# First expert's tokens gathered like the others, eight embedding parts ahead of the experts, and two loads of w_proj_b moved ahead

## The chip, the cores and the metric

The kernel runs on one core of a Trainium2 chip. A core has five engines, each with its own queue that it works off in order: TensorE (PE, matrix products), VectorE (DVE), ScalarE (ACT), GpSimd (POOL) and SyncE (SP). SP, ACT and POOL also issue DMA transfers, which the core's 16 DMA engines carry out. The metric is the device time of one execution in microseconds (us), here the median of several runs. The kernel before takes 1797.73 us (median of 3 runs, 1795.44 to 1806.05).

## The reference

One decoder block: 512 tokens of width 1024, in float32. Two gated linear-attention mixers are merged and projected, and the result is normalised into `x2`. Then a mixture of 32 experts, each token going to its best four, is added to a gate of per-layer embeddings `p`, and the sum is normalised:

```python
ya = o_a @ w_proj_a;  yb = o_b @ w_proj_b
merged = sigmoid(gate_a) * ya + sigmoid(gate_b) * yb
x2 = layer_norm(ALPHA * x + merged @ w_out)          # in words, shortened
top_logit, top_e = lax.top_k(x2 @ w_router + b_router, 4)
top_w = softmax(top_logit)
# for each expert e, on the tokens that chose it:
gate = minimum(hgu[:, :1024], 7.0); up = clip(hgu[:, 1024:], -7.0, 7.0)
act = (up + 1.0) * gate * sigmoid(1.702 * gate)
y += top_w * (act @ w_down[e] + b_down[e])
emb = sigmoid(x2 @ w_ple_gate) * (p @ w_ple_proj)    # 512 x 1024
out = layer_norm(ALPHA * x2 + y + emb)
```

## The kernel before, in words

**The stages.** The first 600 us are the two mixers and the merge. The merge multiplies by `w_proj_b` in two halves of 512 columns; its second half loads two 1 MB pieces (`raw`, L199) through SP, converts each piece on ACT and DVE into two parts (L172, L174) and multiplies them on PE (L182, L184). The results leave PSUM through L935 on DVE. Then `w_out` follows, and for each of the four tiles of 128 tokens the second norm: `second_norm(n)` stores the normed rows `hr` to DRAM (`h_d`, L974) and turns them into `H2` (L980); `logits(n)` (L986) and `choose` (L992 to L1007) find the four best experts of every token.

**The sort.** Experts are sorted by their number of tokens: `sort_experts` (L1128, from `key` L1131 and `tmp` L1133 on) writes each expert's rank, and for every rank a table of token numbers is made by small matmuls (`ptab`, L862) and a few steps on DVE (`tb` L864 to `gidx` L879). Ranks 0 and 1 are the first two experts by number (FIXED), so their tables hang on no ranks, but they stand behind the sort in the code.

**The 32 experts.** Nineteen are long (96 slots for tokens, as blocks of 64 and 32), thirteen short (64 slots). An expert's tokens are fetched from `h_d` by an indirect DMA of POOL (`gather`, L1326) while the expert ahead is computed, and turned by PE and ACT (`ptr`, L1342; `turned`, L1343). The weights, 12 MB for an expert, come through SP in loads of 1 MB (L1318) into 18 buffers that are reused in turn; the buffers of `hr` and `gb` are among them. Every product of the experts has line L1452: `pg` and `pq` up, `po` and `pq` down. The outputs `og` are added to `y_d` in DRAM by POOL (L1596).

**The first expert** is the exception. Its tokens are not gathered: `place(n)` (L1013, 64 matmuls) multiplies `hr` by a one-hot matrix straight into the PSUM banks `px`, which ACT copies to where the tokens belong (L1605). Its products start before the sort is done; the sort, the first tables and gather(1) are in its fourth step (TABLES_AT = 3).

**The embedding parts.** `embed(i)` computes one of 32 pieces of 128 tokens by 128 columns: 8 matmuls of `H2` with `rawg`, 2 of `pT` with `rawp` (L1037, L1039), a sigmoid on ACT (L1041) and a product on DVE (L1042) into `stg`. After four pieces a column is full and POOL adds it to `y_d` (L1044). `stg` has one buffer. Every expert computes one piece between its up and down products; experts 25 and 27 compute two, experts 30 and 31 none. `scaled_rows` (L1237) writes ALPHA times `hr` to `y_d` through a buffer `tmp` that the sort uses too.

**What sets the order.** The program is written once, in the order of the code, and a scheduler then moves instructions by their readiness in its own model; after that each engine's queue is fixed, and an instruction that has to wait holds up all behind it on its engine.

Of the kernel before, what the change touches and what calls it, by code (L numbers as in the profile page):

```python
# [21 lines left out]
P = 128  # L22
S = 512
NT = S // P
D = 1024
# [25 lines left out]

SPLIT_AHEAD = 300
# [7 lines left out]

TABLES_AT = 3
# [34 lines left out]
def block_kernel(ctx: ExitStack, tc: tile.TileContext, a: dict, out: bass.AP):  # L96
# [69 lines left out]
    low_after = []  # L166

    def split_parts(src, shape, tag="w"):
        with tc.high_priority(offset=ahead[0]):
            both = split.tile([P, 2] + shape[1:], F32R, name="parts_" + tag, tag="parts")  # L170
            hi, lo = both[:, 0], both[:, 1]
            s_.activation(hi, src, AF.Copy)  # L172
            with tc.issue_after(low_after.pop()) if low_after else nullcontext():
                v_.tensor_tensor(lo, src, f32(hi), op=ALU.subtract)  # L174
        return hi, lo
# [725 lines left out]
    M = CAP  # L901
# [23 lines left out]
    firsts = [m10[:, i, :] for i in range(4)]  # L925
    nc.sync.dma_start(gates[0], gb_d.rearrange("i p t -> p i t"))
# [5 lines left out]
    for c in range(2):  # L932
# [8 lines left out]
        project(psm, wpb[:, c * 512:(c + 1) * 512], 512, lambda k: oTb[k], "T", ev, (vt, gt) if c == 0 else ())  # L941
# [18 lines left out]
    ohs_f = ep.tile([P, K4 * NE + NT * M], F32, name="ohs_f", tag="xg")  # L960
    oh = ohs_f[:, :K4 * NE].rearrange("p (k e) -> p k e", e=NE)
    ohf = ohs_f[:, K4 * NE:].rearrange("p (n m) -> p n m", m=M)
# [25 lines left out]
    def choose(n0, n1):  # L988
# [17 lines left out]
        for n in range(n0, n1):  # L1006
            chosen = v_.tensor_scalar(ohf[:, n, :], iota_s[:, :M], pos1[:, n, 0:1], None, op0=ALU.is_equal)  # L1007
        return chosen.ins

    def place(n, halves=(0, 1)):  # L1010

        for k in range(halves[0] * 4, halves[-1] * 4 + 4):
            tc.keep_in_program_order(t_.matmul(px[k // 4][:, k % 4, :M], hr[:, n, k * P:(k + 1) * P], ohf[:, n, :],  # L1013
                                               start=False, stop=False))
# [8 lines left out]

    def embed(i):

        n = i % NT
        cs = slice(i // NT * P, (i // NT + 1) * P)
        if n == 0:
            raw = emb["gate"] = plp.tile([P, KD, P], F32, name="rawg", tag="rawg")
            nc.scalar.dma_start(raw, a["w_ple_gate"][0][:, cs].rearrange("(k q) c -> q k c", q=P))  # L1030
            rawp = emb["proj"] = plp.tile([P, 2, P], F32, name="rawp")
            nc.scalar.dma_start(rawp, a["w_ple_proj"][0][:, cs].rearrange("(k q) c -> q k c", q=P))
            emb["out"] = plp.tile([P, NT, P], F32, name="stg")
        t = slice(n * P, (n + 1) * P)
        pg = psm.tile([P, 512], F32, name="ple", tag="att")
        for k in range(KD):
            t_.matmul(pg[:, :P], H2[:, k, t], emb["gate"][:, k, :], start=(k == 0), stop=(k == KD - 1))  # L1037
        for k in range(2):
            t_.matmul(pg[:, P:2 * P], pT[:, k, t], emb["proj"][:, k, :], start=(k == 0), stop=(k == 1))  # L1039
# [61 lines left out]

    px = [psm.tile([P, 4, P], F32, name="px", tag="proj", bufs=4) for _ in range(2)]

    def frame(half, start):

        nothing, one = sel[0:1, 1:2].to_broadcast([1, P]), ones_b[0:1, 0:1].to_broadcast([1, 512])
        t_.matmul(px[half].rearrange("p k m -> p (k m)"), nothing, one, start=start, stop=not start)

    frame(0, True)
    frame(1, True)  # L1110
    choose(0, 2)
    place(0)
# [57 lines left out]
    def first_tables():  # L1170
# [3 lines left out]
        with tc.issue_after(chosen):  # L1174
            sort_experts(pc[:, :NE])
# [505 lines left out]
```

## Time and profile before

| what | us |
|---|---|
| median of 3 runs | 1797.73 |
| the profiled execution | 1802.86 |
| its span in the trace | 1801.1 |
| PE busy | 1725.2 (96% of the span) |
| DVE busy | 557.4 (31%) |
| ACT busy | 409.0 (23%) |
| POOL busy | 196.3 (11%) |

All times in the rows below count from the start of the span. A row of the timeline gives a start, a duration, the engine, the line of the kernel, the operation with its output and inputs, and how many instructions the row takes together; in square brackets stands the idle time of the engine just before it and what the engine waited for ("<-DMA ..." a transfer, "<-PE ..." another engine). The product L1452 on `turned` at 674.58 is the first of expert 0.

### The profile page before, as it was taken

To read this page: it belongs to the slowest core of one execution; us is meant where nothing else is said; L and a number is where in the kernel's file an instruction comes from. 1 tells how busy PE (TensorE), PEld (TensorE's weight loads), DVE (VectorE), ACT (ScalarE), POOL (GpSimd) and SP (SyncE) were. 2 spreads that over 40 slices of the span, in tenths; PEclk is the share of its full clock that TensorE was granted. 3 is DMA by queue.
4 is the path that set the end of the run, shared out by engine and by line. 5 is a ranking of instruction groups with operands and counts; after the bars stand their busy time and mean duration, and the time that the engine had idled before them with its cause. 6 is when DMAs were issued, how large, how long until landed. Compare 5 with 4: busy or idle time off the path is not lost. (4 is left out here: it accounts for less than half of the span.)

```text
span 1801.1 us, 26079 instructions
## 1 busy us (share of the span) xinstructions
PE 1725.2 (96%) x10591; PEld 973.9 (54%) x10591; DVE 557.4 (31%) x1326; ACT 409.0 (23%) x653; POOL 196.3 (11%) x202
## 2 busy tenths in 40 slices
PE   6999999999998999999999999999999999999994
PEld 5888887888886873344343434334343434334422
DVE  7566455436334654111121111111111102102104
ACT  3665455334322321011011011011010101101111
POOL 1000000000000101102011102102010101110113
PEclk9999999999998989999999999999999999999997
DMA  8322232322218477999999999999999998999993
GB/s 267 107 70 71 71 136 99 140 94 71 94 71 297 167 282 300 359 414 356 408 361 406 406 370 355 409 413 380 410 409 388 405 411 316 415 362 412 408 370 133
DMA packets 127642, 513.93 MB, mean 285 GB/s; under 512 B 14434, under 2 KB 44546, under 8 KB 78228
## 3 DMA queue, kind: packets, MB, share of 16 engines
q1 hardware_dynamic: 95988, 466.11, 64.6%
q0 software_dynamic: 16160, 29.63, 6.8%
q10 hardware_dynamic: 15360, 16.39, 2.7%
q8 instruction: 86, 1.41, 0.3%
q14 instruction: 48, 0.39, 0.1%
HBM read 484.36 MB, written 27.72 MB: 284 GB/s over the span
## 5 line engine op out<-in xcount | busy, mean ns | idle before, releaser
L1452 PE MATMUL pg<-raw,turned 128*64 128x512 f32 (+1 forms) x2120 | 423.2, 532 | 4.1 <-DVE up L1502 3.7
L1452 PEld LDWEIGHTS pg<-raw,turned 128*64 128x64 f32 x2120 | 149.4, 137 | 240.6 <-issue 200.9
L1502 DVE TENSOR_SCALAR up<-pg 128x256 f32<-128x256 f32 (+1 forms) x45 | 24.2, 537 | 708.2 <-PE pg L1452 708.2
L1452 PE MATMUL pq<-raw,turned 128*32 128x512 f32 (+1 forms) x2000 | 198.3, 498 | 0.0
L1452 PE MATMUL po<-raw,turned 128*64 128x512 f32 x784 | 175.9, 597 | 0.0
L182 PE MATMUL proj<-parts_w,H 128*128 128x512 f32 x640 | 161.7, 398 | 0.0
L182 PE MATMUL proj<-H,parts_w 128*128 128x512 f32 x640 | 157.4, 394 | 3.3 <-ACT vt L499 1.9
L174 DVE TENSOR_TENSOR parts_w<-raw,parts_w 128x1024 fp32r<-128x1024 f32 x84 | 102.5, 1222 | 154.5 <-ACT parts_w L172 154.0
L1500 ACT ACTIVATE sgs<-pg 128x256 f32<-128x256 f32 (+1 forms) x45 | 21.3, 474 | 543.7 <-PE pg L1452 543.7
L1596 POOL DMA_INDIRECT y_d<-og,sidx x50 | 80.0, 1600 | 526.6 <-ACT og L1587 321.7
L182 PEld LDWEIGHTS proj<-parts_w,H 128*128 128x128 f32 x640 | 121.2, 191 | 25.1 <-DVE H L939 0.3
L182 PEld LDWEIGHTS proj<-H,parts_w 128*128 128x128 f32 x640 | 119.1, 188 | 28.2 <-ACT vt L499 2.3
L172 ACT ACTIVATE parts_w<-raw 128x1024 fp32r<-128x1024 f32 x84 | 88.7, 1059 | 178.0 <-PE proj L184 172.1
L1452 PEld LDWEIGHTS pq<-raw,turned 128*32 128x32 f32 x2000 | 55.3, 109 | 124.3 <-issue 106.6
L1452 PEld LDWEIGHTS po<-raw,turned 128*64 128x64 f32 x784 | 55.1, 138 | 97.7 <-issue 93.3
L184 PE MATMUL proj<-parts_w,H 128*128 128x512 f32 x320 | 84.0, 393 | 0.0
L1326 POOL DMA_INDIRECT xg<-h_d,gidx x49 | 50.4, 1029 | 295.6 <-PE ptr L1342 248.5
L184 PE MATMUL proj<-H,parts_w 128*128 128x512 f32 x320 | 80.5, 390 | 0.0
L1587 ACT ACTIVATE og<-po,wslot 128x512 f32<-128x512 f32 x32 | 22.0, 687 | 214.1 <-PE po L1452 199.9
L184 PEld LDWEIGHTS proj<-parts_w,H 128*128 128x128 f32 x320 | 60.8, 190 | 12.9
L184 PEld LDWEIGHTS proj<-H,parts_w 128*128 128x128 f32 x320 | 59.9, 188 | 12.4
L1037 PE MATMUL ple<-rawg,H 128*128 128x128 f32 x512 | 62.4, 275 | 0.0
(351 smaller groups left out, 1800.0 us busy)
## 6 DMA issues: line engine op xcount, KB each, us to landing
raw<-in_w_gate_up_dram SPq DMA_DIRECT2D x223, 1024.0 KB
raw<-in_w_down_dram SPq DMA_DIRECT2D x98, 1024.0 KB
raw<-in_w_in_dram SPq DMA_DIRECT2D x36, 1024.0 KB
hr<-in_w_gate_up_dram SPq DMA_DIRECT2D x22, 1024.0 KB
hr<-in_w_down_dram SPq DMA_DIRECT2D x20, 1024.0 KB
gb<-in_w_gate_up_dram SPq DMA_DIRECT2D x11, 1024.0 KB
gb<-in_w_down_dram SPq DMA_DIRECT2D x10, 1024.0 KB
raw<-in_w_proj_a_dram SPq DMA_DIRECT2D x4, 1024.0 KB
```

What stands on the lines that cost most here:

```text
L172: s_.activation(hi, src, AF.Copy)
L174: v_.tensor_tensor(lo, src, f32(hi), op=ALU.subtract)
L182: t_.matmul(ps, wh if keep else x, x if keep else wh, start=st, stop=False)
L184: t_.matmul(ps, wl if keep else xh, xh if keep else wl, start=False, stop=stop)
L1037: t_.matmul(pg[:, :P], H2[:, k, t], emb["gate"][:, k, :], start=(k == 0), stop=(k == KD - 1))
L1326: g_.indirect_dma_start(out=columns_of(xg, i), out_offset=None, in_=by_parts(h2_d, parts), in_offset=bass.IndirectOffsetOnAxis(ap=gidx[:, ...
L1452: t_.matmul(dst, x, cols, start=start, stop=stop, skip_group_check=closed)
L1500: s_.activation(dst, gate, AF.Sigmoid, scale=SW_ALPHA)
L1502: v_.tensor_scalar(tmp, up, LIMIT + 1.0, 1.0 - LIMIT, op0=ALU.min, op1=ALU.max)
L1587: s_.activation(columns_of(og, i), (po, pq)[i][:, :D // parts] if i else po, AF.Copy, scale=wslot[:, e, i:i + 1])
L1596: g_.indirect_dma_start(out=by_parts(y_d, parts), out_offset=rows_of(e, i), in_=columns_of(og, i), in_offset=None, compute_op=ALU.add)
```

## The change

- **First expert.** `place`, the banks `px` and their copies are gone. The sort and the first tables come directly behind the choice of the last tile; expert 0 gets its tokens by `gather(0)` and is turned like all others.
- **Embedding parts.** The first eight (two columns) stand in the code between the first tables and expert 0, and the weights of both columns are loaded ahead (`rawg`, `rawp` have two buffers). The other 24 are spread by a formula that gives none to experts 4, 9, 14, 19, 24, 29, 30 and 31 and one to each of the rest.
- **Rows.** `scaled_rows` scales `hr` in place and stores it, without `tmp`.
- **Loads.** The two `raw` pieces of the second half of `w_proj_b` are issued by SP ahead of the loads of `m`, not behind them.
- **Room.** `oh` shrinks, and the program is built with a smaller scratch for DMA descriptors that POOL writes (8192).

The diff, cut to its core:

```diff
+EMBED_FIRST = 8
+EMBED_BUFS = 2
-TABLES_AT = 3
...
+    raws_pb = [ring.tile([P, 4, 512], F32, name="raw", tag="raw") for _ in range(2)]
+    for u in range(2):
+        nc.sync.dma_start(raws_pb[u], wpb[:, 512:].rearrange("(k p) c -> p k c", p=P)[:, 4 * u:4 * u + 4, :])
     nc.sync.dma_start(gates[0], gb_d.rearrange("i p t -> p i t"))
     nc.sync.dma_start(m10, m1_d[:4].rearrange("i p t -> p i t"))
...
-        project(psm, wpb[:, c * 512:(c + 1) * 512], 512, lambda k: oTb[k], "T", ev, (vt, gt) if c == 0 else ())
+        project(psm, wpb[:, c * 512:(c + 1) * 512], 512, lambda k: oTb[k], "T", ev, (vt, gt) if c == 0 else raws_pb)
...
     choose(0, 2)
-    place(0)
     second_norm(2)
     logits(2)
     second_norm(3)
-    place(1, (0,))
     choose(2, 3)
     logits(3)
-    place(1, (1,))
-    place(2, (0,))
-    chosen = choose(3, 4)
-    place(2, (1,))
-    low_after += [chosen] * 3
-    for half in range(2):
-        place(3, (half,))
-        frame(half, False)
+    choose(3, 4)
...
     def scaled_rows():
 
         for n in range(NT):
-            tmp = ep.tile([P, D], F32, name="tmp", tag="og")
-            s_.activation(tmp, hr[:, n, :], AF.Copy, scale=ALPHA)
-            nc.scalar.dma_start(y_d[n * P:(n + 1) * P, :], tmp)
+            s_.activation(hr[:, n, :], hr[:, n, :], AF.Copy, scale=ALPHA)
+            nc.scalar.dma_start(y_d[n * P:(n + 1) * P, :], hr[:, n, :])
...
     def embeds(e):
 
-        while len(done) < min(e + 1 + (e >= NE - 7) + (e >= NE - 5), NE):
+        while len(done) < min(EMBED_FIRST + -(-(e + 1) * (NE - EMBED_FIRST) // (NE - 2)), NE):
             embed(len(done))
             done.append(e)
...
-            if e == 0 and k == TABLES_AT:
-                first_tables()
-                xg = gather(1)
-                main_tables(2)
...
-    for half in range(2):
-        s_.activation(xs[:, half * 4:half * 4 + 4, :], px[half][:, :, :M], AF.Copy)
+    embed_weights(0)
+    embed_weights(1)
+    first_tables()
+    xg0 = gather(0)
     scaled_rows()
+    for i in range(EMBED_FIRST):
+        embed(i)
+        done.append(i)
+    turn_tokens(xg0, 0)
     for e in range(NE):
-        if e % 2 == 0 and 0 < e < NE - 2:
+        if e % 2 == 0 and e < NE - 2:
...
-    nc = bacc.Bacc("TRN2", target_bir_lowering=False, num_devices=1)
+    nc = bacc.Bacc("TRN2", target_bir_lowering=False, num_devices=1, dynamic_dma_scratch_size=8192)
```

**PE, from the choice of the last tile to the products of expert 0.** Before, the products of expert 0 (`pg`, `pq` on `turned_9427`) stand around the first matmul that needs the sort (`pord`) and around the small table matmuls (`ptab`):

```order
L1452 MATMUL pg<-raw,turned_9427 64x512 x12
L1143 LDWEIGHTS facts
L1143 MATMUL pord<-sel_by,facts 1x32
L1452 MATMUL pg<-raw,turned_9427 64x512 x4
L1452 MATMUL pq<-raw,turned_9427 32x512 x9
L862 LDWEIGHTS ohs
L862 MATMUL ptab<-facts,ohs 128x3
L1452 MATMUL pq<-raw,turned_9427 32x512
```

In the changed program the same place on PE reads as follows. The row `ptab` of 128x3 stands 32 times (16 for token numbers, 16 for weights), the pair of `ple` rows eight times and `ptab` of 128x6 sixteen times:

```order
L1122 MATMUL pord<-sel_by,facts 1x32
L861 LDWEIGHTS ohs
L861 MATMUL ptab<-facts,ohs 128x3
...
L1035 MATMUL ple<-rawg,H_9433 128x128 x8
L1037 MATMUL ple<-rawp,pT 128x128 x2
...
L1319 MATMUL ptr<-ident,xg 128x128 x6
...
L861 MATMUL ptab<-facts,ohs 128x6
L1429 MATMUL pg<-raw,turned_9427 64x512 x16
L1429 MATMUL pq<-raw,turned_9427 32x512 x16
```

Behind `pord` and in front of the embedding parts now stand all 32 table matmuls; expert 0's products stand behind the parts and behind the turning of its gathered tokens (`ptr`).

**ACT, at the last two tiles' norms.** With the semaphores that each row waits for: before, the store of the normed rows of tile 2 (`h2_d`, the DRAM rows `h_d`), the copies into `H2`, the scaled rows to `tmp`, and the same for tile 3:

```order
L974 DMA h2_d_62<-hr_9054 128x1024 [waits DMAHW0_49,DVE_49]
L980 ACTIVATE H2_9433<-pt_9806 128x4x128 [waits PE_49]
L980 ACTIVATE H2_9433<-pt_9812 128x4x128 [waits PE_49]
L1241 ACTIVATE tmp_9921<-hr_9054 128x1024 [waits DMAHW4_49]
L1242 DMA y_d_63<-tmp_9921 128x1024 [waits DMAHW2_49,Activation_49]
L974 DMA h2_d_62<-hr_9054 128x1024 [waits DVE_49]
L980 ACTIVATE H2_9433<-pt_9838 128x4x128 [waits PE_49]
```

and in the changed program:

```order
L973 DMA h2_d_62<-hr_9054 128x1024 [waits DMAHW1_49,DVE_49]
L979 ACTIVATE H2_9433<-pt_9792 128x4x128 [waits PE_49]
L979 ACTIVATE H2_9433<-pt_9798 128x4x128 [waits PE_49]
L1218 ACTIVATE hr_9054<-hr_9054 128x1024 [waits DMAHW1_49]
L973 DMA h2_d_62<-hr_9054 128x1024 [waits DMAHW4_49,DVE_49]
L979 ACTIVATE H2_9433<-pt_9824 128x4x128 [waits PE_49]
```

The scaling of tile 2 (L1218) overwrites the rows that the store of tile 2 reads, and waits for the semaphore that this store sets (DMAHW1); the copies of tile 3 stand behind it.

**ACT, at the second column of the first eight parts**, in the changed program (`stg_9997` is the first column, `stg_10051` the second, in the same buffer):

```order
L1039 ACTIVATE stg_9997<-ple_10037 128x128 [waits PE_49]
L1020 DMA rawp_10269<-in_w_ple_proj_dram 128x2x128 [waits DMAHW7_49]
L1039 ACTIVATE stg_10051<-ple_10052 128x128 [waits DMASW4_49,DVE_49,PE_49]
L1039 ACTIVATE stg_10051<-ple_10065 128x128 [waits PE_49]
L1039 ACTIVATE stg_10051<-ple_10078 128x128 [waits PE_49]
L1018 DMA rawg_11274<-in_w_ple_gate_dram 128x8x128 [waits DMAHW0_49,PE_49]
L1039 ACTIVATE stg_10051<-ple_10091 128x128 [waits PE_49]
L1320 ACTIVATE turned0_9427<-ptr_10105 128x4x2x64 [waits PE_49]
L1320 ACTIVATE turned0_9427<-ptr_10111 128x2x4x32 [waits PE_49]
```

The first sigmoid of the second column waits for DMASW4, the semaphore of the DMA by which POOL adds the first column to `y_d`; the copies of expert 0's tokens stand behind the four sigmoids. Before, one column took four experts, and no such rows stood ahead of expert 0.

## Rows read from the trace of the kernel before

**Rows 1.** Waits of PE from 720 us on, first row: total us, times, longest.

```profile
PE ptr L1342 <- DVE sgs L1504: 10.4, 10, 1.0
```

**Rows 2.** Windows: stretch, sum, engines' busy us, granted clock, DMA share, GB/s.

```profile
1025.00:1050.00 25.00, 23.96 (x140) 8.27 (x136) 3.66 (x7) 2.20 (x5) 0.00 (x0) 1.00 1.02 422
```

**Rows 3.** Waits of SP's queue from 720 us on: total us, times, longest.

```profile
SPq L1318 <- DMA rawg<-in_w_ple_gate_dram: 132.6, 7, 23.1
```

**Rows 4.** Timeline of ACT, second half of w_proj_b.

```profile
571.62 2.00 ACT L172 ACTIVATE parts_w<-raw 128x1024 fp32r<-128x1024 f32 x2 [13.91 <-PE proj L184]
574.34 1.06 ACT L172 ACTIVATE parts_w<-raw 128x1024 fp32r<-128x1024 f32 x1 [0.71 <-DMA raw<-in_w_proj_b_dram]
```

**Rows 5.** Timeline of PE, start of the second half of w_proj_b.

```profile
575.83 0.47 PE L182 MATMUL proj<-oTl,parts_w 128*128 128x512 f32 x1 [2.89 <-DVE gb L935]
...
577.41 0.63 PE L182 MATMUL proj<-oTl,parts_w 128*128 128x512 f32 x1
...
580.39 0.47 PE L182 MATMUL proj<-oTh,parts_w 128*128 128x512 f32 x1
```

**Rows 6.** Timeline of ACT, norms of tiles 2 and 3.

```profile
657.03 0.33 ACTq L974 DMA_DIRECT2D h_d<-hr  x1
...
663.40 1.09 ACT L980 ACTIVATE H<-pt 128x512 f32<-128x512 f32 x2 [3.15 <-PE pt L979]
670.87 1.06 ACT L1241 ACTIVATE tmp<-hr 128x1024 f32<-128x1024 f32 x1 [6.38 <-DMA y_d<-tmp]
```

**Rows 7.** Timeline of DVE, choice of the last tile, sort, first tables.

```profile
667.24 0.20 DVE L992 MAX8 top<-plg 128x8 f32<-128x32 f32 x1 [1.89 <-PE plg L986]
...
668.72 0.18 DVE L999 CAST mask_b<-mask 128x32 bf16<-128x32 f32 x1
...
679.96 1.22 DVE L1133 TENSOR_TENSOR tmp<-key 128x1024 f32<-128x1024 f32 x1 [5.51 <-DMA y_d<-tmp]
...
694.26 0.17 DVE L864 COPY tb<-ptab 128x12 f32<-128x12 f32 x1 [1.55 <-PE ptab L862]
```

**Rows 8.** Timeline of PE, from the last logits to expert 2, and expert 8.

```profile
663.63 1.03 PE L1013 MATMUL px<-ohs_f,hr 128*128 128x96 f32 x8
...
674.58 5.37 PE L1452 MATMUL pg<-raw,turned 128*64 128x512 f32 x24
...
696.02 0.56 PE L862 MATMUL ptab<-facts,ohs 128*128 128x3 bf16 x16
...
707.31 1.95 PE L1037 MATMUL ple<-rawg,H 128*128 128x128 f32 x16
...
709.54 0.40 PE L1342 MATMUL ptr<-ident,sgs 128*128 128x128 f32 x2
...
717.07 0.87 PE L1342 MATMUL ptr<-ident,xg 128*128 128x128 f32 x6
...
722.43 5.37 PE L1452 MATMUL pg<-raw,turned 128*64 128x512 f32 x24
...
759.17 5.32 PE L1452 MATMUL pg<-raw,turned 128*64 128x512 f32 x24
...
949.12 2.11 PE L1452 MATMUL pg<-raw,turned 128*64 128x512 f32 x8
...
988.44 4.08 PE L1452 MATMUL pg<-raw,turned 128*64 128x512 f32 x18
```

**Rows 9.** Tile y_d: waits until a transfer (us, times), and landing times.

```profile
  DMA y_d<-stg: 43.8, 5
...
DMA to landing us min/median/max: 8.3/9.6/16.3
```

**Rows 10.** Tile stg: landing of its own transfers, as far as seen.

```profile
DMA to landing us min/median/max: 16.3/16.3/16.3
```

**Rows 11.** Timeline of DVE and of PE, one embedding part in a short expert.

```profile
1350.40 0.42 DVE L1504 SCALAR_TENSOR_TENSOR sgs<-pg,sgs 128x256 f32<-128x256 f32 x1
...
1351.82 0.40 PE L1342 MATMUL ptr<-ident,sgs 128*128 128x128 f32 x2
```

More of the change, by code (lines that the diff above doesn't have):

```diff
@@ L1 @@
 import math
-from contextlib import ExitStack, nullcontext
+from contextlib import ExitStack
 import concourse.bass as bass
@@ L172, in split_parts @@
             s_.activation(hi, src, AF.Copy)
-            with tc.issue_after(low_after.pop()) if low_after else nullcontext():
-                v_.tensor_tensor(lo, src, f32(hi), op=ALU.subtract)
+            v_.tensor_tensor(lo, src, f32(hi), op=ALU.subtract)
         return hi, lo
@@ L959, in block_kernel @@
     nc.gpsimd.dma_start(ptile, a["p"][0, 0].rearrange("(n q) d -> q n d", q=P))
[L960 to L962 removed]
+    oh = ep.tile([P, K4, NE], F32, name="oh", tag="xg")
     ohv = oh.rearrange("p (n k) e -> p n e k", n=NT)
@@ L1005, in choose @@
                                 op0=ALU.add, op1=ALU.mult)
[L1006 to L1014, printed above, removed]
     wos = {}
@@ L1022, in block_kernel, with embed_weights @@
     emb = {}
+    def embed_weights(c):
+        cs = slice(c * P, (c + 1) * P)
+        raw = plp.tile([P, KD, P], F32, name="rawg", tag="rawg", bufs=EMBED_BUFS)
+        nc.scalar.dma_start(raw, a["w_ple_gate"][0][:, cs].rearrange("(k q) c -> q k c", q=P))
+        rawp = plp.tile([P, 2, P], F32, name="rawp", bufs=EMBED_BUFS)
+        nc.scalar.dma_start(rawp, a["w_ple_proj"][0][:, cs].rearrange("(k q) c -> q k c", q=P))
+        emb[c] = raw, rawp
     def embed(i):
-        n = i % NT
-        cs = slice(i // NT * P, (i // NT + 1) * P)
+        n, c = i % NT, i // NT
+        cs = slice(c * P, (c + 1) * P)
+        if c not in emb:
+            embed_weights(c)
         if n == 0:
[L1029 to L1032, printed above, removed]
             emb["out"] = plp.tile([P, NT, P], F32, name="stg")
+        gate, proj = emb[c]
         t = slice(n * P, (n + 1) * P)
@@ L1100, in block_kernel @@
         add_out(0, {n: ps[n]})
[L1102 to L1110, printed above, removed]
     choose(0, 2)
-    place(0)
     second_norm(2)
@@ L1468, in rows_down @@
             return wd_e[:, 2 * u * P:(2 * u + 2) * P, :].rearrange("o (p j) d -> p (o j) d", j=2)
-        xg = gather(e + 1) if 0 < e < NE - 1 else None
+        xg = gather(e + 1) if e < NE - 1 else None
         first, *more = blocks(e)
@@ L1546, in expert @@
         if e == NE - 2:
-            lasts["bias"] = plp.tile([P, D], F32, name="bb3", tag="rawg")
+            lasts["bias"] = plp.tile([P, D], F32, name="bb3", tag="rawg", bufs=EMBED_BUFS)
             lasts["gain2"] = plp.tile([P, NT, P], F32, name="stg").rearrange("p n c -> p (n c)")
@@ L1553, in expert @@
             spread(lasts["bias"], a["ln_moe_b"][0])
-        while len(done) < min(e + 1 + (e >= NE - 7) + (e >= NE - 5), NE):
-            embed(len(done))
-            done.append(e)
+        embeds(e)
         if not last:
```

9 lines of the change are left out of this document (3 added, 6 removed).

## The prediction

> **What bounds the kernel now.** I read the windows first, then the waits of PE, then the timelines around the two places that the change touches. In the stretch of the experts PE is busy almost all the time, 23.96 of 25 us in a typical window, and the DMA engines are at a share of 1.02 there [rows 2]: PE is the bound, the weight stream runs close behind it. Yet the waits of PE from 720 us on name no weight load; the longest row is 10.4 us behind DVE's `sgs` [rows 1]. So work taken from PE inside the experts shortens the kernel as long as the loads keep up. Ahead of the experts it is otherwise: there a chain of choice, sort, tables and transfers decides when expert 0 can start, and today PE passes over it, since expert 0 starts at 674.58 while the sort begins at 679.96 only [rows 7, 8].
>
> **The change, step by step. Times are on the clock of the profiled execution.**
>
> *w_proj_b.* PE stands still for 2.89 us at 575.83 behind L935 on DVE [rows 5]. DVE is late because it converts pieces that ACT could only take at 571.62, and the next at 574.34, when the load landed [rows 4]. The idle time of 13.91 at 571.62 is put down to PE, but three buffers for parts had come free by then, so I take this for the first piece's landing. Loads issued ahead of `m` land earlier; what stays is the emptying of one PSUM bank, some 0.7 us by estimate, so 2.2 of the 2.89 go. Behind the idle time seven matmuls from 577.41 to 580.39 last up to 0.63 and need 2.98 us, twice the usual, that is the lower of PE's two clock levels [rows 5]; without the idle time 1.5 more go. Gain 3.7; the bounds are nothing and 4.4 (all idle time and the clock). PE is busy from there to the logits, so what is won here arrives at them.
>
> The two pieces came 2.7 us apart [rows 4], close to the 2.5 us that 1 MB takes at the 422 GB/s of [rows 2], so they came one behind the other and not mixed with all else; that is why I let them profit from an earlier place. The Trainium skill, page "DMA: Bandwidth & Descriptors", section "Issuing engines are not separate DMA queues", says that transfers of SP, ACT and POOL run on the same 16 engines and interleave whoever starts them. By that, POOL's loads issued in the same microseconds would keep the pieces late; the gain would be nothing and the sum below 3.7 us higher.
>
> *ACT at tile 3.* Scaling in place waits for the store of tile 2, issued at 657.03 [rows 6]. Stores to `y_d` land after 8.3 to 16.3 us, median 9.6 [rows 9]; I take 9.6, so the scaling can start at 666.6. It takes 1.06, and the copies of tile 3 stand behind it and behind another issue of 0.33: they start at 668.0 instead of 663.40 [rows 6]. From there to the choice on DVE were 3.84 us [rows 6, 7], of which `place` held PE for 1.03 [rows 8]. The choice comes at 670.9 instead of 667.24. Bounds: 669.6 (landing in 8.3), and 666.2 if the store is done before.
>
> *Sort and tables.* The mask is done 1.66 after the choice [rows 7]; counting and `key` I put at 0.5. The sort's `tmp` no longer waits for `y_d<-tmp` (5.51 idle before it [rows 7]) and starts at 673.1, 6.9 earlier than now. From `tmp` to the table copy `tb` are 14.3 us, of which 1.55 is a wait for table matmuls stuck between products of expert 0 [rows 7]; they are alone now, so `tb` comes at 685.8. The last 16 table matmuls end 2.3 after it (696.02 with 0.56 against 694.26 [rows 7, 8]): 688.1. From some 671 to there PE has almost nothing: this is the cost of giving up `place`.
>
> *The eight parts.* In PE's new order they stand behind all 32 table matmuls, so they cannot fill that hole. One part is 2.23 us, 707.31 to 709.54 [rows 8]; eight are 17.8, and 1.5 more for the low clock after the idle time (the same as at 577 us [rows 5]). PE ends them at 707.5. Gather(0) is hidden under them: issued at some 688, even 16.3 us [rows 9] would bring it by 705. But the fourth part ends at 698.5, sigmoid and product take 0.6 by estimate, and then POOL adds the first column to `y_d`; the first sigmoid of the second column waits for that, and behind it on ACT stand the copies of expert 0's tokens. This transfer is seen to land once, in 16.3 us [rows 10]; POOL's later transfers waited for such ones 43.8/5 = 8.8 us on average [rows 9], and stores to `y_d` have the median 9.6. With the weight buffers full, little else is moved then, so I take 10.2: landing at 709.3. Four sigmoids, transposes (0.87 for six of them [rows 8]) and the copies add some 2.8: expert 0 starts at 712.1. Less the 3.7 from above that is 708.4, **33.8 later than 674.58.**
>
> *Expert 0.* It becomes like expert 1. Today 674.58 to 722.43 is 47.85, expert 1 to 759.17 is 36.74 [rows 8]: **minus 11.1.** Hidden tables and 3 us of waits for the sort are in this.
>
> *Parts among the experts.* Eight are gone. The six in short experts (4, 9, 14, 19, 24, 29) covered a wait: `sgs` is done at 1350.82, the transposes behind the part start at 1351.82 [rows 11], so at least 1.0 of 2.23 goes; the next bias products move into the gap, so I take 1.35 each, 8.1 (bounds 6.0 and 13.4). The second parts in experts 25 and 27 stood behind a first one and covered nothing: 4.5. **Minus 12.6.**
>
> *Order of products.* Expert 8, 949.12 to 988.44, is 39.3 because PE changes between `pg` and `pq` at every weight piece, 2.6 more than expert 1 with the same work [rows 8]. In the new order it runs nearly like expert 1; others change little. **Minus 2.5** (bounds 0 and 3).
>
> *Free.* Scaling in place costs ACT what `tmp` did, hidden after the choice. The weights of the first two columns are loaded ahead, during the sort. The smaller descriptor scratch: bounds nothing and one wait of POOL for a transfer, 8.8 us [rows 9], which is hidden under an expert for each gather but the first; I take nothing.
>
> **Sum.** 33.8 - 11.1 - 12.6 - 2.5 = +7.6. On the profiled execution's 1802.86 that is 1810.5; it lies 5.1 above the median of 1797.73, so against the median I predict **1805**, 0.4% above, which a measurement of this kernel hardly tells from no change (about 1% is what it can).
>
> **The rivals.**
>
> *The weight stream becomes the bound (slower).* Behind expert 1 the change makes PE 15.1 us faster (12.6 + 2.5), while the DMA share is already 1.02 [rows 2], and SP's loads waited 132.6 us for semaphores shared with slow `rawg` loads [rows 3], which remain. If nothing of the 15.1 is kept, the sum is 33.8 - 11.1 = +22.7: 1820, 1.3% slower. It counts as slower once 10.4 of the 15.1 come back as waits of PE. Against it: PE waits for no load now, all 18 buffers are full when expert 0 starts late, and one column's loads fewer fall behind it. Chance 0.12.
>
> *The column's transfer lands late.* With 16.3 [rows 10] instead of 10.2, and the low clock once more after PE's wait: +6.1 + 1.5, so 1813. It needs DMA traffic like that in the middle of the experts. Chance 0.20.
>
> *The hole is filled after all.* If the first parts ran beside the sort, expert 0 would start when gather(0) has landed: issue 688, 9.6 later 697.6, turned at 699.3, less 3.7: 695.6, +21.0 - 26.2 = -5.2: 1792.5. Against it stands PE's fixed order. Chance 0.04.
>
> *No gain at w_proj_b.* The other transfers issued with the two pieces hold them as late as now: 1809. Chance 0.06.
>
> **How the numbers follow.** The forecast has 0.55, between 1798 and 1811 by the bounds of its terms (store of tile 2, 3 less to 2 more; parts in short experts 5 less; clock and landing 3 either way). The remaining 0.03 are several at once. The range 1793 to 1818 takes in the late column and half the hole and leaves out the weight-bound case. Slower by over 1% means above 1815.7: the weight-bound case's 0.12, and 0.05 of late column and low clock together, 0.17. Faster by over 1%, below 1779.8, no case gives; 0.03 for what I do not see. Within 1%: 0.80.
>
> **What would show it.** PE idle for some 15 us or more between the logits and the first `ple`; ACT waiting before the scaling of tile 2 for `h_d<-hr`; ACT waiting before the fifth sigmoid for `y_d<-stg`; first `pg` on turned tokens near 708; expert 0 as long as expert 1, about 37; no wait of PE for a weight load later; no 2.9 us at w_proj_b. I am wrong if the first `pg` comes before 700 or after 716, or if PE waits for weights among experts 15 to 29, where the stream is tightest.

## The result and the profile after

The changed kernel takes **1813.02 us** (median of 4 runs, 1811.38 to 1814.67) against 1797.81 for the kernel before (4 runs, 1795.44 to 1806.05): a ratio of **1.0074 [1.0049, 1.0098]**. It is slower by 0.7%, within the 1% that I counted as no change, and 8 us above the 1805 that I predicted: by the medians 15.2 slower, twice the 7.3 of the forecast. Its profiled execution took 1811.38 us (span 1809.6) against 1802.86 before: +8.5, where my sum said +7.6. That the sum came out so near is luck: two of its terms were wrong by about the same amount (5.9 and 7.5), in opposite directions.

The way through the experts is read from the first `pg` product of some of them:

| | before [rows 8] | after | later by |
|---|---|---|---|
| expert 0 starts | 674.58 | 702.53 | 27.9 (predicted 33.8) |
| expert 1 starts | 722.43 | 739.20 | 16.8: expert 0 is 11.2 shorter (predicted 11.1) |
| expert 31 starts | 1751.43 (not among the rows above) | 1760.62 | 9.2: 30 experts gave back 7.6 (predicted 15.1) |
| end of the span | 1801.1 | 1809.6 | 8.5 |

The timeline of PE after the change. Columns: start, duration, engine, line, operation, count, and in brackets the idle time before it and what ended it. An f32 product counts as two there: the eight products of a part with `rawg` stand as x16.

```profile
572.34 0.39 PE L181 MATMUL proj<-oTl,parts_w 128*128 128x512 f32 x1
...
575.29 0.39 PE L181 MATMUL proj<-oTh,parts_w 128*128 128x512 f32 x1
...
660.55 1.92 PE L985 MATMUL plg<-wrw,H 128*128 128x32 f32 x8 [2.65 <-ACT H L979]
...
669.86 0.18 PE L1122 MATMUL pord<-sel_by,facts 32*1 32x32 bf16 x1 [3.63 <-DVE sel_by L1120]
676.06 0.19 PE L861 MATMUL ptab<-facts,ohs 128*128 128x3 bf16 x1 [6.02 <-DVE ohs L852]
...
680.96 0.59 PE L861 MATMUL ptab<-facts,ohs 128*128 128x3 bf16 x16 [2.26 <-DVE gidx L878]
681.41 3.76 PE L1035 MATMUL ple<-rawg,H 128*128 128x128 f32 x16
...
685.61 1.95 PE L1035 MATMUL ple<-rawg,H 128*128 128x128 f32 x16
...
701.24 0.82 PE L1319 MATMUL ptr<-ident,xg 128*128 128x128 f32 x6
...
702.53 7.09 PE L1429 MATMUL pg<-raw,turned 128*64 128x512 f32 x32
...
855.18 0.50 PE L1319 MATMUL ptr<-ident,sgs 128*128 128x128 f32 x2 [0.65 <-DVE sgs L1481]
...
864.22 1.08 PE L1429 MATMUL pg<-raw,turned 128*64 128x512 f32 x4 [0.19 <-ACT turned L1320]
...
1135.76 1.05 PE L1429 MATMUL pq<-raw,turned 128*32 128x512 f32 x2
1136.74 1.94 PE L1429 MATMUL pg<-raw,turned 128*64 128x512 f32 x8
1138.61 1.92 PE L1429 MATMUL pq<-raw,turned 128*32 128x512 f32 x14
1140.45 1.94 PE L1429 MATMUL pg<-raw,turned 128*64 128x512 f32 x8
1142.32 1.06 PE L1429 MATMUL pq<-raw,turned 128*32 128x512 f32 x8
1143.32 1.94 PE L1429 MATMUL pg<-gb,turned 128*64 128x512 f32 x8
```

The second half of w_proj_b starts at 572.34 with no idle time, against 575.83 after 2.89 idle [rows 5]. From the last logits at 660.55 PE has almost nothing until the first part at 681.41; that part's 16 take 3.76, those of the later parts 1.95: PE works at the lower of its two clock levels. The parts end at 701.24 and the tokens of expert 0 follow at once.

ACT in the same stretch, then DVE and POOL:

```profile
565.95 2.21 ACT L172 ACTIVATE parts_w<-raw 128x1024 fp32r<-128x1024 f32 x2 [8.67 <-DMA raw<-in_w_proj_b_dram]
...
649.94 0.34 ACTq L973 DMA_DIRECT2D h_d<-hr  x1
...
658.95 1.06 ACT L1218 ACTIVATE hr<-hr 128x1024 f32<-128x1024 f32 x1 [6.83 <-DMA h_d<-hr]
...
659.92 0.58 ACT L979 ACTIVATE H<-pt 128x512 f32<-128x512 f32 x1
...
698.56 0.45 ACT L1039 ACTIVATE stg<-ple 128x128 f32<-128x128 f32 x2 [5.77 <-DMA y_d<-stg]
```

```profile
664.32 0.20 DVE L991 MAX8 top<-plg 128x8 f32<-128x32 f32 x1 [6.71 <-PE plg L985]
...
666.56 1.22 DVE L1112 TENSOR_TENSOR tmp<-key 128x1024 f32<-128x1024 f32 x1
...
679.20 0.15 DVE L863 COPY tb<-ptab 128x12 f32<-128x12 f32 x1
```

```profile
693.42 1.44 POOL L1042 DMA_DIRECT2D y_d<-stg  x1 [7.98 <-DVE stg L1040]
```

Both waits that I forecast on ACT are there: the scaling of tile 2 waits for the store `h_d<-hr`, issued at 649.94 and seen at 658.95 (9.0 later, I took 9.6); the fifth sigmoid waits for the first column, `y_d<-stg`, issued at 693.42 and landed by 698.56 (5.1 later, I took 10.2 and feared 16.3).

Windows (stretch, sum, busy us of PE, PEld, DVE, ACT, POOL, granted clock, DMA share, GB/s):

```profile
570.00:590.00 20.00, 20.00 (x90) 16.53 (x89) 11.03 (x15) 6.52 (x8) 0.00 (x0) 1.00 0.87 322
635.00:640.00 5.00, 5.00 (x17) 4.32 (x16) 2.15 (x10) 0.00 (x0) 0.00 (x0) 0.50 0.28 113
640.00:645.00 5.00, 5.00 (x21) 4.02 (x21) 1.30 (x2) 1.06 (x1) 0.00 (x0) 0.90 0.36 133
...
650.00:675.00 25.00, 11.05 (x70) 9.31 (x68) 15.86 (x48) 6.95 (x9) 1.46 (x1) 0.59 1.01 402
675.00:700.00 25.00, 20.23 (x181) 19.86 (x182) 10.93 (x44) 1.83 (x7) 4.81 (x3) 0.79 0.44 122
1025.00:1050.00 25.00, 25.00 (x152) 6.62 (x151) 1.40 (x12) 1.97 (x4) 3.59 (x3) 1.00 1.02 408
```

PE is busy 11.05 of the 25 us from 650 on, and the clock comes back only in the next window. From the experts on nothing has changed in kind [rows 2].

Waits of PE behind 702 us and of SP behind 720 us (total us, times, longest):

```profile
PE ptr L1319 <- DVE sgs L1481: 13.3, 15, 1.0
...
PE pg L1429 <- ACT turned L1320: 1.4, 4, 0.6
PE pbr L162 <- DMA bb<-in_ln_moe_b_dram: 0.5, 1, 0.5
```

```profile
SPq L1295 <- DMA rawg<-in_w_ple_gate_dram: 80.5, 4, 21.8
```

No row of PE names an expert's weights, so the stream of weights is not the bound; SP's wait for `rawg` even fell from 132.6 [rows 3] to 80.5. The wait for `sgs` rose from 10.4 [rows 1] to 13.3, and one for `turned` came. Expert by expert, the 10.4 are ten waits of 1.04 in the ten long experts that change between `pg` and `pq` at every weight piece; of the 13.3, 9.4 are nine of these and 3.9 are new, 0.65 in each of the six short experts without a part: only these are gaps that the parts used to fill.

### The profile page after: what moved, and what is told of

It is laid out like the page before. It is cut to its first block, busy times and chain, and to the rows that moved or that the text cites. A ratio compares the mean times of both kernels' runs of the same rounds, so it can differ in the third digit from the quotient of the medians.

```text
span 1809.6 us, 25948 instructions
## 1 busy us (share of the span) xinstructions
PE 1720.2 (95%) x10529; PEld 973.6 (54%) x10529; DVE 557.7 (31%) x1322; ACT 409.5 (23%) x653; POOL 198.4 (11%) x204
## 5 line engine op out<-in xcount | busy, mean ns | idle before, releaser
L1429 PE MATMUL pg<-raw,turned 128*64 128x512 f32 (+1 forms) x2120 | 417.4, 530 | 5.3 <-DVE up L1479 3.7
L183 PE MATMUL proj<-H,parts_w 128*128 128x512 f32 x320 | 80.5, 390 | 0.0
L183 PEld LDWEIGHTS proj<-H,parts_w 128*128 128x128 f32 x320 | 59.9, 188 | 12.4
```

The source lines that it names most:

```text
L183: t_.matmul(ps, wl if keep else xh, xh if keep else wl, start=False, stop=stop)
L1429: t_.matmul(dst, x, cols, start=start, stop=stop, skip_group_check=closed)
```

## The experiments

Each ratio is against the kernel before, run beside it on the same chip. "Expert 0" and "expert 31" mean the start of that expert's first `pg`. Before and after, these are 674.6 and 1751.4, and 702.5 and 1760.6.

| kernel | us | ratio | expert 0 | expert 31 |
|---|---|---|---|---|
| loads_only | 1799.69 | 0.9983 [0.9969, 0.9997] | 669.6 | 1749.7 |
| rows_later | 1816.05 | 1.0077 [1.0055, 1.0100] | 702.7 | 1762.3 |
| in_hole | 1815.51 | 1.0073 [1.0050, 1.0095] | 702.6 | 1763.5 |
| long_free | 1829.63 | 1.0152 [1.0129, 1.0174] | 703.5 | 1775.4 |
| loads_batched | 1789.17 | 0.9925 [0.9909, 0.9941] | 669.0 | 1731.3 |
| after_batched | 1792.18 | 0.9944 [0.9927, 0.9961] | 705.9 | 1733.8 |
| hole4 | 1815.49 | 1.0078 [1.0057, 1.0098] | 699.2 | 1760.3 |
| none_first | 1810.69 | 1.0057 [1.0035, 1.0080] | 689.2 | 1757.9 |
| soft_first | 1809.79 | 1.0056 [1.0039, 1.0073] | 698.7 | 1756.8 |
| hole_soft | 1804.08 | 1.0020 [1.0003, 1.0036] | 693.5 | 1751.2 |
| no_loads | 1815.74 | 1.0094 [1.0066, 1.0122] | 704.0 | 1762.5 |
| before_scratch | 1798.85 | 0.9993 [0.9978, 1.0007] | 676.2 | 1753.0 |

**The loads of w_proj_b alone (loads_only), and everything but them (no_loads).** The first adds the two early loads to the kernel before; the second takes them out of the changed one.

```diff
+    raws_pb = [ring.tile([P, 4, 512], F32, name="raw", tag="raw") for _ in range(2)]
+    for u in range(2):
+        nc.sync.dma_start(raws_pb[u], wpb[:, 512:].rearrange("(k p) c -> p k c", p=P)[:, 4 * u:4 * u + 4, :])
...
-        project(psm, wpb[:, c * 512:(c + 1) * 512], 512, lambda k: oTb[k], "T", ev, (vt, gt) if c == 0 else ())
+        project(psm, wpb[:, c * 512:(c + 1) * 512], 512, lambda k: oTb[k], "T", ev, (vt, gt) if c == 0 else raws_pb)
```

> The kernel before with one edit of the change alone: the two loads of w_proj_b's second half issued ahead of m. Theory: the pieces land early, PE's idle 2.89 us and the low clock behind it go (about 5 us at that place, and some 2 more in w_out, as in the changed kernel), all of it arrives at expert 0, since place() starts that expert straight from the logits: 1791, about 7 below the kernel before. Rival (the transfers interleave, or the gain is hidden by the chain behind it): 1797 to 1798, PE still idle 2 to 3 us there, or expert 0 starting at 674 as before.

> The changed kernel with the two loads of w_proj_b back behind the loads of m: the change without this part. Theory: PE idles 2.9 us again at the second half of w_proj_b and works at the low clock behind it, 5 us in all, and some 2 more follow in w_out, all in front of the sort: expert 0 at 707 to 709.5 instead of 702.5, ratio to the kernel before 1.010 to 1.012. Rival (the part is worth nothing in this kernel): expert 0 at 702 to 703, 1.0075.

Put in alone, the loads bring expert 0 forward by 5.0, but only 0.2% of the time is gained, less than half of the 7 us that I expected: at expert 31 the lead is 1.7, and 1.5 of what is lost is expert 30 alone, in which the clock fell (0.66 from 1730 to 1740 us). Taken out, expert 0 comes only 1.5 later, not 4.5 or more. In no_loads the stall is back: ACT's row at 571.54 (whose idle time this time names the DMA, so my reading of 571.62 in [rows 4] is confirmed) and PE's at 575.75:

```profile
571.54 2.01 ACT L172 ACTIVATE parts_w<-raw 128x1024 fp32r<-128x1024 f32 x2 [13.55 <-DMA raw<-in_w_proj_b_dram]
```

```profile
575.75 0.47 PE L181 MATMUL proj<-oTl,parts_w 128*128 128x512 f32 x1 [2.53 <-DVE gb L933]
```

Yet the clock did not fall behind it, and neither did it fall from 635 to 645, where it fell in the changed kernel. The windows of no_loads:

```profile
570.00:590.00 20.00, 17.47 (x77) 13.98 (x76) 13.25 (x17) 7.66 (x9) 0.00 (x0) 1.00 0.87 318
635.00:640.00 5.00, 5.00 (x37) 4.66 (x37) 1.90 (x4) 1.60 (x3) 0.00 (x0) 1.00 0.82 289
640.00:645.00 5.00, 5.00 (x24) 4.10 (x23) 3.25 (x10) 1.06 (x1) 0.00 (x0) 1.00 0.37 130
```

So the restart at 575.75 instead of 572.34 costs 3.4, and the clock gives back 5 x (0.50 + 0.10) = 3.0 of it by 645. At their place the loads are worth the 3.4; what arrives later depends on where the clock falls, and the two ratios (1.0094 and 1.0074) can't tell the kernels apart.

**The order on ACT (rows_later, soft_first).** In rows_later the scalings of tiles 2 and 3 stand behind the copies of tile 3; in soft_first the exponential of the softmax (a function `exponents` of its own, called ahead of the tables) stands ahead of both scalings too. `held_by` is the last copy of tile 3 in the one and the exponential in the other.

```diff
-            s_.activation(hr[:, n, :], hr[:, n, :], AF.Copy, scale=ALPHA)
+            with tc.issue_after(held_by) if n > 1 else nullcontext():
+                s_.activation(hr[:, n, :], hr[:, n, :], AF.Copy, scale=ALPHA)
...
+    held_by = exponents()
     first_tables()
```

> The changed kernel with the scaling of hr for tiles 2 and 3 put behind the copies of tile 3 on ACT (an order edge), so that these copies no longer stand behind a wait for the store of tile 2. Theory: the wait of ACT (6.83 us before the scaling of tile 2) holds up the last logits by 3 to 4 us and costs PE its clock; without it the sort and expert 0 start 3 to 5 us earlier: 1808 to 1810. Rival (the last choice waits for something else): expert 0 at 702 as in the changed kernel, 1813.

> The changed kernel with the softmax's exponential and then the scaling of tiles 2 and 3 behind the copies of tile 3 on ACT. In rows_later the choice of the last tile came some 3 us earlier, but the exponential, now behind two scalings that wait for stores, made DVE wait 1.6 us in front of the ranks, and the low clock lasted 1.0 longer. Theory: with the exponential ahead of the scalings nothing on DVE waits any more, the sort starts 2 to 3 us earlier than in the changed kernel and expert 0 at 699 to 700.5 instead of 702.5: ratio to the kernel before 1.005 to 1.007. Rival (another wait takes its place): expert 0 at 702 or later.

In rows_later the sort's first step `tmp` starts 2.3 earlier (664.22), but the exponential now stands behind two scalings that wait for stores, and DVE waits for it in the middle of the sort:

```profile
667.03 0.17 DVE L1169 TENSOR_REDUCE sm<-ex 128x4 f32<-128x16 f32 x1 [1.58 <-ACT ex L1167]
```

and the low clock lasted into the second part:

```profile
680.71 3.76 PE L1036 MATMUL ple<-rawg,H 128*128 128x128 f32 x16
...
685.11 2.60 PE L1036 MATMUL ple<-rawg,H 128*128 128x128 f32 x16
```

Expert 0 starts no earlier. With the exponential first (soft_first) `tmp` starts at 662.63, the first part at 677.49, and expert 0 at 698.7, 3.8 earlier than in the changed kernel. The stall costs what I said, but it takes both moves to have it back. A part of the 3.8 is luck of the clock: in soft_first it stays at 1.00 from 635 to 645, and tile 3 is copied 1.6 earlier (654.74) than in rows_later (656.34), which fell to the low level there.

**Filling the hole (in_hole, hole4, hole_soft).** Five (four) of the parts are written between the sort's ranks and `pord`; hole_soft has four there and soft_first's order.

```diff
+        for i in range(HOLE):
+            embed(i)
         pn = psm.tile([P, 512], F32, name="pord", tag="att")
...
+    scaled_rows()
     first_tables()
     xg0 = gather(0)
-    scaled_rows()
-    for i in range(EMBED_FIRST):
+    for i in range(HOLE, EMBED_FIRST):
```

> The changed kernel with five of the first eight embedding parts written into the sort, ahead of the matmul pord, and the scaled rows written ahead of the tables (they must be stored before a column is added to them). Theory: PE is idle some 15 us during the sort and the tables, the parts take 2.23 us each and can run there, so expert 0 starts as soon as the gathered tokens have landed, at 690 to 693 instead of 702.5: 1802 to 1804, still above the kernel before. Rival 1 (gather or tables come later because DVE and POOL have the parts' work in front): 698 to 702, 1809 to 1813. Rival 2 (the parts in the hole bring the whole gain that was meant): below 1798.

> The changed kernel with only the first four parts (one column) written into the sort; the second column stays behind the tables. In the run with five parts there, the fifth part's product on DVE waited for the first column's transfer and held up the table copy for 4.8 us. Theory: without that wait the table copy comes some 4 us earlier, PE has four parts less behind the tables, and expert 0 starts at 696 to 698 instead of 702.6: ratio to the kernel before 1.002 to 1.005. Rival (the gather's landing, or the second column's wait for the first one's transfer, now sets the start): expert 0 at 700 to 703, ratio 1.007.

> The same order on ACT and the first four parts written into the sort (as hole4). Theory: both gains add up, expert 0 starts at 695.5 to 697 instead of 702.5 (699.2 with the four parts alone), ratio to the kernel before 1.003 to 1.006; still above the kernel before, since the chain from choice to gather is longer than place() was. Rival: the start is bound by the gather's landing or the second column: 699 or later.

With five the first part runs at 667.33, but the fifth opens the second column, whose sigmoid on ACT waits for the first column's transfer. Its product stands on DVE ahead of the table copy `tb`, and PE waits for the next table:

```profile
688.30 0.29 DVE L1041 TENSOR_TENSOR stg<-ple,stg 128x128 f32<-128x128 f32 x1 [4.78 <-ACT stg L1040]
688.51 0.16 DVE L864 COPY tb<-ptab 128x12 f32<-128x12 f32 x1
```

```profile
691.30 0.59 PE L862 MATMUL ptab<-facts,ohs 128*128 128x3 bf16 x16 [8.04 <-DVE facts L1150]
691.75 3.76 PE L1036 MATMUL ple<-rawg,H 128*128 128x128 f32 x16
```

Nothing is won. With four, expert 0 starts 3.4 earlier, with the order of soft_first 9.1 earlier, at 693.5: that is the start of my rival "the hole is filled" (695.6), but the time is then 1804.08, still 0.2% above the kernel before, and not the rival's 1792.5: the experts gave back less than it counts on, and its profiled execution reaches expert 31 at 1751.2, before at 1751.4. In hole4 the 3.4 dwindled over the experts: the same 32 small products of expert 11, at 1104.78 in the changed kernel and at 1102.35 in hole4, are

```profile
1104.78 1.90 PE L1429 MATMUL pq<-hr,turned 128*32 128x256 f32 x32
```

```profile
1102.35 2.37 PE L1432 MATMUL pq<-hr,turned 128*32 128x256 f32 x32
```

Their order in the program is the same; why they run 0.5 slower in one stays open.

**The parts ahead at all (none_first), and where they are missing later (long_free).** none_first takes the eight parts from the start and spreads them over the experts as before; long_free frees six long experts (`NO_EMBED`) of their part instead of six short ones.

```diff
-EMBED_FIRST = 8
+EMBED_FIRST = 0
...
+NO_EMBED = (5, 10, 13, 17, 22, 27)
-        while len(done) < min(EMBED_FIRST + -(-(e + 1) * (NE - EMBED_FIRST) // (NE - 2)), NE):
+        while len(done) < min(EMBED_FIRST + e + 1 - sum(x <= e for x in NO_EMBED), NE):
```

> The changed kernel with no part ahead of expert 0 and the parts spread as in the kernel before (one in each expert to 29, two in 25 and 27). Theory: the eight parts ahead cost what they take (702.5 less the gather's landing and turning at some 693: 9 to 10 us) and save only about 6 among the experts, since in a short expert a part costs no more than 0.5 us: some 3 to 4 us faster than the changed kernel, ratio to the kernel before 1.004 to 1.006. Rival (a part costs its 2.23 us wherever it stands): eight parts are 17.8 us more among the experts, 8 us slower than the changed kernel, ratio 1.012.

> The changed kernel with six long experts (5, 10, 13, 17, 22, 27) left without an embedding part instead of the six short ones 4, 9, 14, 19, 24, 29; all else the same, 8 parts ahead. Theory: in a short expert a part covers PE's wait for the activation, so that taking it away brought only 0.1 to 0.8 us each; in a long expert a part covers some 0.5 us, so taking it away there brings about 1.7: 6 x 1.3 = 8 less, 1805. Rival (a part costs PE the same wherever it stands, and the small saving is the order of the products): 1813.

none_first starts expert 0 13.3 earlier than the changed kernel and expert 31 only 2.8 earlier: eight parts cost 13.3 at the start and save some 10.5 behind it. The other 14.6 of the 27.9 by which expert 0 starts late are what giving up `place` costs, less what the loads give. Moving the parts gains nothing (2.8 are lost by expert 31, which the two ratios can hardly tell apart): ahead of expert 0 they stand on the path at full price and partly at the low clock, and among the experts some of them were cheap.

long_free failed as a test of that price: the freed long experts 5, 13, 17 and 27, whose up products stand as in the changed kernel, are shorter by 1.4, 0.7, 1.0 and 1.0, but 10 and 22, freed too, are longer by 0.3 and 0.8, and other experts' products changed their order (PE changes 208 times between `pg` and `pq` in the up projections of the long experts 1 to 30, 188 times in the changed kernel, 194 before, 54 in loads_batched), PE is busy 1732.8 us instead of 1720.2 with the same 10529 matmuls, and the kernel is 0.8% slower than the changed one by the two ratios.

**The order of products (loads_batched, after_batched).** The products of the up projection of long experts 1 to 30 keep the order of the code: 32 `pg`, 32 `pq`, twice, instead of what the scheduler makes of it (`keep` is set for them). One is loads_only with this, the other the changed kernel with this.

```diff
-            t_.matmul(dst, x, cols, start=start, stop=stop, skip_group_check=closed)
+            mm = t_.matmul(dst, x, cols, start=start, stop=stop, skip_group_check=closed)
+            if keep:
+                tc.keep_in_program_order(mm)
```

> The kernel before with the two loads of w_proj_b moved ahead, and with the up products of the long experts 1 to 30 held in the order of the code: four weight pieces for pg, the same four for pq, then the other four; the scheduler had taken them piece by piece (pg, pq, pg, pq) from expert 8 on. Theory: the change of products costs PE itself 2.9 us in such an expert (39.4 against 36.5), not the weights' arrival; 13 experts give some 35 us, of which the weight stream, at a DMA share of 1.02, lets through about half to two thirds: ratio to the kernel before 0.984 to 0.990. Rival (the alternation follows the arrival of the weights, and PE waits for them instead): ratio 0.997 to 1.0, with new waits of PE for weight loads.

> The changed kernel with the same order held in the long experts 1 to 30, nothing else. Theory: what the change saved among the experts (fewer parts) was eaten by another order of the products, above all the form 'pg of one piece, two matmuls of pq, pg of the next', 0.8 us dearer than the plain alternation; with the order held, expert 1 to expert 31 takes about 25 to 35 us less than in the changed kernel, and the ratio to the kernel before is 0.988 to 0.995. Rival (the weight stream is the bound there): ratio above 1.0, PE waiting for weight loads.

Both beat both kernels; loads_batched is the fastest, 0.75% below before, though short of the 0.984 to 0.990 that I expected. Its long experts from 8 on are 36.5 to 37.2 long (13 and 17: 36.7 and 37.2) instead of 39.1 to 40.0, where nothing else binds. From after to after_batched the way from expert 1 to 31 shortens by 30.1.

Not all of this is the products. In expert 13 of the kernel before, its first `pg`, the row behind its last `pq`, and the transposes are

```profile
1121.78 1.94 PE L1452 MATMUL pg<-raw,turned 128*64 128x512 f32 x8 [0.34 <-ACT turned L1343]
...
1144.69 0.41 PE L1452 MATMUL pg<-brows,sel_by 128*64 128x512 bf16 x2
1146.13 0.74 PE L1342 MATMUL ptr<-ident,sgs 128*128 128x128 f32 x4 [1.04 <-DVE sgs L1504]
```

and in loads_batched the first `pg` and the transposes

```profile
1109.30 5.37 PE L1455 MATMUL pg<-raw,turned 128*64 128x512 f32 x24
...
1130.48 0.74 PE L1345 MATMUL ptr<-ident,sgs 128*128 128x128 f32 x4
```

The products take 22.91 with 15 changes and 21.18 with 3, 1.7 more. Another 1.0 is a wait: in the alternating order the last `pg` ends just ahead of the last eight `pq`, and DVE needs longer than these for `sgs`; with all 32 `pq` behind the last `pg` it is done in time. The ten waits of 1.04 [rows 1] are gone in loads_batched (no row of its waits names `sgs`), and PE is busy 1706.1 us instead of 1725.2.

In loads_batched the weights now hold PE up, and at the end a load of the last norm that comes behind them, as its waits show:

```profile
PE pg L1455 <- DMA raw<-in_w_gate_up_dram: 17.3, 9, 5.0
PE pbr L161 <- DMA bb<-in_ln_moe_b_dram: 6.5, 1, 6.5
```

and a window in which PE idles and its clock falls:

```profile
1200.00:1250.00 50.00, 42.62 (x298) 19.52 (x296) 4.50 (x20) 4.88 (x11) 9.52 (x8) 0.90 0.95 358
```

So my rival "the weight stream becomes the bound" is real, but it took an order that frees some 30 us of PE to meet it, twice the 15.1 that I reckoned with. after_batched waits for weights only 5.0 us, probably because its expert 0 starts 36.9 later and the buffers have that much longer to fill; no run shows it apart.

**The scratch (before_scratch).** The kernel before with the change's smaller descriptor scratch:

```diff
-    nc = bacc.Bacc("TRN2", target_bir_lowering=False, num_devices=1)
+    nc = bacc.Bacc("TRN2", target_bir_lowering=False, num_devices=1, dynamic_dma_scratch_size=8192)
```

> The kernel before with the smaller scratch for POOL's descriptors (8192) and nothing else. Theory: POOL never has enough descriptors under way to wait for room, ratio 0.999 to 1.001. Rival (POOL waits for room, gathers and additions come later): ratio above 1.003, POOL's indirect transfers longer than the 1.0 and 1.6 us of the kernel before.

0.9993 [0.9978, 1.0007]: no effect, as I had it.

## Why the prediction was right, and where it was not

| step | predicted | measured |
|---|---|---|
| restart of w_proj_b | 2.2 of idle, 1.5 of clock | 3.5 and 1.6 (575.83 to 572.34; 580.39 to 575.29) |
| choice (`MAX8`) | 670.9 - 3.7 = 667.2 | 664.32 |
| sort (`tmp`) | 673.1 - 3.7 = 669.4 | 666.56 |
| last of the 32 table matmuls ends | 688.1 - 3.7 = 684.4 | 681.55 |
| parts end | 707.5 - 3.7 = 703.8 | 701.24 |
| landing of the first column | 10.2 | 5.1 |
| expert 0 starts | 708.4 (+33.8) | 702.53 (+27.9) |
| expert 0 | -11.1 | -11.2 |
| parts in six short experts | -8.1 | -2.8 |
| doubles in 25 and 27 | -4.5 | -2.2 and -1.4 (27 lost 0.8 to its order) |
| order of products | -2.5 | -1.4 in expert 8; +0.7 to 0.8 in each of 13, 17, 22 and 28 |

**What held.** The mechanism at the start held step by step: the stall of ACT behind the store, a hole of PE between logits and parts, the low clock in the first part (4.20 from 681.41 to 685.61 instead of 2.23, so 2.0 more; I had 1.5), the eight parts on the path, expert 0 as long as expert 1. The rivals "late column" and "weight stream" did not come, and none_first shows that the parts ahead gain nothing even by themselves.

**The start was 5.9 too late.** 2.6 of it stand already at the end of the parts. w_proj_b gave 7.0 by the end of w_out and not 3.7: no load was left to wait for, so all the idle time went, and from 635 to 650 the clock happened to be low for less long than before. I let the emptying of a PSUM bank stay (0.7) and it did not show. Of these 3.3 some was lost again, as the logits behind the stall ran at the low clock (1.92 for eight, 660.55). The other 3.3 are the column: it landed in 5.1, so nothing followed the parts but the turning of tokens (1.3 and not 4.6). I had reasoned that little else is moved then, yet took a price near the median of all landings in `y_d`. The row of the wait was right, its price was not. Nor was a quiet stretch shown to be the reason: later columns of the changed kernel landed in 4.5 and 4.9 among the experts too (last section).

On w_proj_b I had weighed a rule of the Trainium skill (page "DMA: Bandwidth & Descriptors", section "Issuing engines are not separate DMA queues"), that transfers interleave whichever engine started them; by that, those of other engines would have kept the pieces late. Here ACT's first piece was there at 565.95 and not at 571.54, so moving the loads ahead on their own queue brought them 5.6 forward. No run here mixes the queues on purpose.

**The experts gave back 7.6 and not 15.1.** The step that failed is "the next bias products move into the gap, so I take 1.35 each". The six short experts without part became shorter by 0.83, 0.56, 0.42, 0.55, 0.10 and 0.38, 2.8 in all. Part of the gap stayed (0.65 at 855.18), and the bias products that moved into it had covered another wait: behind four of the six PE now waits for ACT's `turned` (0.19 at 864.22, 1.4 in all). A part in a short expert costs 0.1 to 0.8 of its 2.23; one in a long expert 0.7 to 1.4 (long_free), a second one behind another its full price (25 became 2.2 shorter; 27 1.4, with 0.8 lost to the next point), as I had it. The 7.6 are these 2.8, 3.6 of the doubles, 1.4 of expert 8, less 3.2 in 13, 17, 22 and 28 (next point), and some 2.9 in eight other experts, 0.1 to 0.5 each, among them some whose products stand as before (2, 6, 15). In these three the difference sits in one group of small products with 256 columns (in 2: 3.79 instead of 4.22; in 15: 3.56 instead of 4.00), like the 0.5 of hole4; why they run at two speeds stays open.

**The order of products.** I read that expert 8 loses 2.6 by changing between `pg` and `pq`, and took the change to mend it there and nowhere to harm. Nor were the 2.6 all PE's own: 1.04 of them was the wait for `sgs` that stands in [rows 1]. The change mended 1.4 of the 2.6, that wait and 0.4 of products, and in 13, 17, 22 and 27 put 2 and 14 `pq` in place of 8 and 8 (28 has two changes more). The rows at 1135.76 show why that costs: two `pq` hold PE for 0.98 until the next `pg`, as long as eight do. Beside this, what the order held in all was twelve times my term: 30 us, in nearly all long experts from 8 on. I had looked at the one expert whose order the change touched. The Trainium skill, page "TensorEngine Tiling (Array Packing)", section "Key Properties", says that changing the tiling mode drains TensorE. The traces agree that a change costs: `pg` works on tiles of 128x64 and `pq` on tiles of 128x32, and the up products of expert 13 take 21.18 with 3 changes (loads_batched) and 22.91 with 15 (before), so some 0.14 us a change in groups of eight. The count alone is not the price: experts 11 and 23 are nearly as long with 9 changes (39.4) as 13 with 15 (39.6), without a wait for `sgs` but with a group of two `pq` among theirs.

**The median.** Against the profiled execution of before I was 0.9 off (1810.5 against 1811.38). The 1805 subtracted 5.1 because that execution lay so far above its median, and supposed that after would be drawn alike. It was not: after's profiled execution lies below its median. The runs of the kernel before, 21 on one chip, lie between 1793.8 and 1807.5 with mean granted clocks from 0.984 to 0.990, and fall by 1.5 us for each 0.001 of clock (correlation -0.87; 17 earlier ones on the same chip: 1.7 us, -0.92; 11 on another chip: 1.5 us, -0.67). A busy PE at half clock would give 1.8: a stretch of 3.6 us loses 1.8 us of work and takes 0.001 off the mean over 1800 us. After's four runs all lie from 0.979 to 0.982. So the spread of before goes with its clock, about as much as a half clock would give, and the changed kernel has a lower one. That the clock is the cause of the spread is argued from these numbers; no run sets it. Why it falls more often in some executions of before I cannot say; the trace is of one execution each.

## What to carry to other kernels

Work that fills a hole is free only if the engine's written order lets it start before the hole ends, and if nothing it issues (here a sigmoid behind a transfer, a product on DVE ahead of a table copy) stands in front of the chain that made the hole. A piece of work in a pipelined loop is worth what its experts shorten by when it is gone, and that has to be measured by taking it out, since what moves into its place uncovers the next wait. Where products of two tile shapes alternate, look over the whole loop at the size of the groups and at the wait behind the last one: here the order held 30 us, more than all that this change moved.

## What the runs showed of the hardware that I had not expected

- Two `pq` products of 128x32 tiles alone between `pg` products take 0.98 us, the same as eight (0.98 from 1135.76 for two; 1.00 from 1142.32 for eight); 14 take 1.84. Eight run as two groups of four side by side: in the kernel before, in expert 8, four start from 951.16 to 951.18 and four from 951.61 to 951.63. The two alone start at 1135.76 and 1136.22, as far apart as the groups.
- Transfers that add a column to DRAM (`y_d<-stg`) landed in 4.5 to 5.0 us or in 11.2 to 16.9, and the DMA share does not tell which: in the changed kernel 5.0 at 693.42, but also 4.5 at 991.27 and 4.9 at 1335.82, at shares of 1.11 and 0.96 over the 6 us from there; 12.4 at 828.87 and 16.9 at 1507.80, at 0.99 and 1.05. The one seen before took 16.3 [rows 10]. What decides is open.
- After a stretch in which PE was mostly idle, 16 products took 3.76 instead of 1.95. After a single gap of 2.9 us the clock fell in the kernel before [rows 5]; after one of 2.53 in no_loads it did not.
- The clock fell between 635 and 650 while PE was busy all the time (5.00 of 5.00 us at 0.50), in 12 of the 14 kernels; ahead of it stood many small logit products (128x32). In no_loads and soft_first it stayed at 1.00. What tells them apart is open.
